# mLSTM head ends: two-step denominators, mean of the head norm on GpSimd, one more pause ahead of the transposes

## The chip, the cores and the metric

The kernel runs on one core of a Trainium2 chip. The metric is the device time of one execution in microseconds (us), given as the median of several runs. The engines are TensorE (PE; its weight loads are shown apart as PEld), VectorE (DVE), ScalarE (ACT), GpSimd (POOL) and SyncE (SP), which issues transfers. Each engine works through its own instructions in order, and semaphores tie the engines together.

## The reference

One layer of a bidirectional encoder on 512 tokens of width 1024, float32 in and out. A normed input goes through one projection whose columns are shared by four HGRN2 heads and four mLSTM heads. Each runs forward and backward over the sequence, each head's result is normed and gated, and an out-projection joins them. Cross-attention to 256 memory tokens and a squared-ReLU MLP follow. The parts that the change touches are these:

```python
def head_rmsnorm(h, g, n_heads):
    ...
    h32 = h32 * lax.rsqrt(jnp.mean(h32 * h32, axis=-1, keepdims=True) + NORM_EPS)

# mlstm_scan
den = jnp.sum(scores, axis=-1) + w_inter * jnp.einsum('bhtd,bhd->bht', qc, n_st)
h_out = num / jnp.maximum(jnp.abs(den), jnp.exp(-m_t))[..., None]

# reference
x = x + token_mixer(rmsnorm(x, norm_mix[l]), ...)
x = x + cross_attention(rmsnorm(x, norm_xattn[l]), rmsnorm(mem, norm_mem[l]), ...)
x = x + squared_relu_mlp(rmsnorm(x, norm_mlp[l]), ...)
```

## The kernel before, in words

Every large product is made of three matmuls (`mm3`, lines 261 to 263): both operands are split into a high and a low part, and high by high, high by low and low by high are summed in PSUM. Weights stream from memory through SyncE's queue, and later ones through GpSimd's (L1102), as blocks of 128 x 1024 into `st` or other buffers. `split_out` (L258) makes their high part `wh` on ScalarE and their low part `wl` on VectorE. There are three buffers each of `st`, `wh` and `wl`. Projections accumulate in four PSUM banks named `mm`; everything small uses four banks named `sm`.

The heads are Python generators. They wait in a list, `chains`; `tick()` is called at fixed places inside the projections and advances one of the first two chains to its next `yield`. A `yield` is thus a pause, in which the program places projection matmuls. Heads run in pairs: HGRN2 0 and 1, 2 and 3, then mLSTM 0 and 1 (here heads 4 and 5) and mLSTM 2 and 3 (heads 6 and 7). The first mLSTM pair runs beside the key and value projections of the memory, the second beside those and the out-projection's first part, where `drain()` finishes them. From what is written, a scheduler sets the final order of instructions on each engine by its own estimates, so an edit in one place can move instructions elsewhere.

An mLSTM chain adds masks and takes exponentials of its gates (L777 to L787), makes scores and states (L793 to L815), and then goes through four tiles of 128 tokens, `wt`. For each, the group of matmuls at L827 writes numerator and denominator of both directions to PSUM. L832 to L834 form max(|den|, e) on VectorE, L836 takes the reciprocal, L838 (ScalarE) and L839 (VectorE) scale and add the two directions. There is a pause after every second tile. Then `head_out` ends the head, as it does for the HGRN2 heads: ScalarE squares each tile and sums it (L592), `rstd_of` makes the mean on VectorE (L197) and its power -0.5 on GpSimd (L199), VectorE multiplies (L594), a pause follows, TensorE transposes four tiles (L601), VectorE applies gain and gate (L602), and the result is split for the out-projection.

`rstd_of` has ten uses: the eight heads, with four numbers on each partition, and the two tiles of memory rows, with one. For the latter ScalarE sums squares (L906), VectorE adds two halves (L908), `rstd_of` follows, VectorE scales the 128 x 1024 tile (L910), and TensorE transposes it (L919).

Of the kernel before, what the change touches and what calls it, by code (L numbers as in the profile page):

```python
# [14 lines left out]
ALU = mybir.AluOpType  # L15
# [10 lines left out]
EPS = 1e-6  # L26
# [54 lines left out]
def trunk(ctx: ExitStack, tc: tile.TileContext, x, mem, wpk, vec, cst, lmask, rmask, rows, out):  # L81
# [5 lines left out]
    v, sc, gp, pe = nc.vector, nc.scalar, nc.gpsimd, nc.tensor  # L87
# [12 lines left out]
    def smb():  # L100
        return pss.tile([P, 512], F32, tag="sm", name=nm("sm"))
# [92 lines left out]

    def rstd_of(ss, w, n):
        ms = tiny(w)
        v.tensor_scalar(out=ms, in0=ss, scalar1=1.0 / n, scalar2=EPS, op0=ALU.mult, op1=ALU.add)  # L197
        r = tiny(w)
        gp.tensor_tensor(out=r, in0=ms, in1=nh.to_broadcast([P, w]), op=ALU.pow)  # L199
        return r, ms  # L200
# [385 lines left out]
    def head_out(o, gate, gcol, idx):  # L586

        junk = T2()
        ss = tiny(4)
        for t in range(4):  # L590
            z = slice(t * P, t * P + P)
            sc.activation(junk[:, z], o[:, z], AF.Square, accum_out=ss[:, t:t + 1])  # L592
        r, _ = rstd_of(ss, 4, P)
        v.tensor_tensor(out=o[:, 0:512].rearrange("p (t e) -> p t e", e=P),  # L594
                        in0=o[:, 0:512].rearrange("p (t e) -> p t e", e=P),
                        in1=r.unsqueeze(2).to_broadcast([P, 4, P]), op=ALU.mult)
        yield
        ps = smb()
        for t in range(4):
            z = slice(t * P, t * P + P)  # L600
            pe.transpose(ps[:, z], o[:, z], ident)  # L601
        v.scalar_tensor_tensor(out=gate, in0=ps, scalar=vc[:, gcol:gcol + 1], in1=gate, op0=ALU.mult, op1=ALU.mult)  # L602
        ys[idx] = hl(YT1())
        split_out(ys[idx][0], ys[idx][1], gate)
        yield
# [161 lines left out]
    def mlstm_chain(h, gate):  # L767
# [7 lines left out]
        for dr in range(2):  # L775
# [5 lines left out]
                            in1=cm.unsqueeze(1).to_broadcast([P, 4, P]), op=ALU.add)  # L781
# [16 lines left out]
        for dr in range(2):  # L798
            v.tensor_tensor(out=kw(dr).rearrange("p (w e) -> p w e", e=P), in0=ap(pk, dr * P, [P, 3], [1, P]),
                            in1=ex(0, dr, dr, h, 3).unsqueeze(2).to_broadcast([P, 3, P]), op=ALU.mult)  # L800
# [18 lines left out]
        for wt in range(4):  # L819
# [9 lines left out]
            e2 = ap(em, wt * 8 + h, [4, 2], [1, 1])  # L829
            nd = tiny(2)  # L830
            n3 = nd[:, :].unsqueeze(2)
            v.tensor_scalar(out=n3, in0=den, scalar1=-1.0, scalar2=None, op0=ALU.mult)  # L832
            v.tensor_tensor(out=n3, in0=n3, in1=den, op=ALU.max)
            v.tensor_tensor(out=n3, in0=n3, in1=e2, op=ALU.max)  # L834
            rd = tiny(2)
            v.reciprocal(rd, nd)  # L836
            z = slice(wt * P, wt * P + P)
# [62 lines left out]
    for t in range(2):  # L900
# [6 lines left out]
        ss = tiny(1)  # L907
# [555 lines left out]
```

## Time and profile before

| | |
|---|---|
| median of three runs | 829.23 us (829.09 to 829.29) |
| profiled execution | 829.61 us, of which the span from first to last instruction is 827.6 us |
| TensorE busy | 814.7 us, 98% of the span |
| VectorE, ScalarE, GpSimd busy | 590.6, 435.2, 77.7 us |
| mean granted TensorE clock | 0.997 |

Busy time counts an engine's instructions but not its waiting. A wait is put down to the instruction that ended it, as the profile infers from semaphores. L numbers are lines of the kernel. The HGRN2 heads end between about 145 and 225 us from the start of the span, the memory rows are normed near 232 us, heads 4 and 5 end near 289 to 296 us, and heads 6 and 7 near 334 to 341 us.

### The profile page before, as it was taken

How to read it: one execution, taken by the hardware profiler on the slowest of the kernel's cores; microseconds unless marked ns; L12 is line 12 of the kernel's file. 1: busy time of each engine (PE TensorE's matmuls, PEld its weight loads, DVE VectorE, ACT ScalarE, POOL GpSimd, SP SyncE). 2: the span in 40 equal slices, each digit the busy share in tenths (PEclk: the TensorE clock that was granted, in tenths of full speed). 3: DMA queues.
4: the chain of work that ended last, by engine and by line, in shares of the span. 5: the costliest groups of instructions: out<-in, count | busy, mean ns of one | idle time of the engine just before them, and what ended most of it. 6: DMA issues, size and time to landing. Idle time of an engine off the chain costs nothing.

```text
span 827.6 us, 12644 instructions
## 1 busy us (share of the span) xinstructions
PE 814.7 (98%) x4862; PEld 677.0 (82%) x4862; DVE 590.6 (71%) x1046; ACT 435.2 (53%) x791; POOL 77.7 (9%) x131
## 2 busy tenths in 40 slices
PE   8999999999999999999999999999999999999996
PEld 6788778877878988887888888888888888888885
DVE  6568975699479888545668985676568566756685
ACT  5247574546578485445455575443454345434544
POOL 2000000100010000100100004012102210220001
PEclk9999999999999999999999999999999999999998
DMA  7332223322342334532343349969836982798332
GB/s 277 118 116 94 78 79 104 101 88 81 102 128 77 128 128 152 148 96 89 106 124 72 83 126 305 254 166 272 224 101 182 280 207 94 187 295 204 105 74 101
DMA packets 34125, 118.91 MB, mean 144 GB/s; under 512 B 3921, under 2 KB 4049, under 8 KB 34066
## 3 DMA queue, kind: packets, MB, share of 16 engines
q1 hardware_dynamic: 22832, 77.80, 27.6%
q0 software_dynamic: 10944, 39.85, 21.7%
q8 instruction: 38, 0.62, 0.3%
q10 hardware_dynamic: 290, 0.47, 0.2%
q14 instruction: 21, 0.17, 0.1%
HBM read 116.00 MB, written 2.10 MB: 143 GB/s over the span
## 4 chain that ended last, share of the span: by engine, by line
PE 85%; issue 6%; DVE 5%; ACT 2%; DMA 1%; POOL 1%; POOLq 0%; ACTq 0%; DVEq 0%
PE mm L261 17%; PE mm L263 17%; PE mm L262 17%; PE sm L1154 6%; PE sm L1155 6%; PE sm L1153 6%; PE mm L1154 2%; PE mm L1153 2%; PE mm L1155 2%; PE sm L827 1%; DVE wl L258 1%; PE sm L562 1%; PE sm L485 1%; ACT wh L258 1%; PE sm L263 1%
## 5 line engine op out<-in xcount | busy, mean ns | idle before, releaser
L258 ACT ACTIVATE wh<-st 128x1024 fp32r<-128x1024 f32 x131 | 138.7, 1060 | 185.0 <-PE mm L262 117.4
L261 PE MATMUL mm<-xT,wh 128*128 128x512 f32 x544 | 215.5, 397 | 0.0
L258 DVE TENSOR_TENSOR wl<-st,wh 128x1024 fp32r<-128x1024 f32 x131 | 160.1, 1223 | 77.3 <-ACT wh L258 76.8
L263 PE MATMUL mm<-xT,wl 128*128 128x512 f32 x544 | 212.9, 391 | 0.1
L262 PE MATMUL mm<-xT,wh 128*128 128x512 f32 x544 | 212.5, 391 | 0.2 <-DVE xT L975 0.2
L263 PEld LDWEIGHTS mm<-xT,wl 128*128 128x128 f32 x544 | 102.2, 188 | 21.8 <-DVE wl L258 0.3
L262 PEld LDWEIGHTS mm<-xT,wh 128*128 128x128 f32 x544 | 102.3, 188 | 20.8 <-DVE xT L975 0.9
L261 PEld LDWEIGHTS mm<-xT,wh 128*128 128x128 f32 x544 | 102.2, 188 | 20.8 <-ACT wh L258 0.3
L1102 POOL DMA_DIRECT2D as<-in_wpk x52 | 39.6, 763 | 250.0 <-DVE wl L258 165.0
L1342 DVE SCALAR_TENSOR_TENSOR t<-mm,rg 128x512 f32<-128x512 f32 x32 | 22.0, 690 | 52.2 <-PE mm L263 52.0
L1155 PE MATMUL sm<-wh,yT 128*128 128x512 f32 x128 | 49.8, 389 | 0.0
L1154 PE MATMUL sm<-wl,yT 128*128 128x512 f32 x128 | 49.8, 389 | 0.0
L1153 PE MATMUL sm<-wh,yT 128*128 128x512 f32 x128 | 49.8, 389 | 0.0
L258 ACT ACTIVATE wh<-as 128x1024 fp32r<-128x1024 f32 x26 | 27.6, 1062 | 37.0 <-PE sm L1155 23.7
L258 DVE TENSOR_TENSOR wl<-as,wh 128x1024 fp32r<-128x1024 f32 x26 | 31.9, 1225 | 14.0 <-ACT wh L258 14.0
L1153 PE MATMUL sm<-wh,a 128*128 128x512 f32 x84 | 32.9, 391 | 0.0
L1155 PE MATMUL sm<-wh,a 128*128 128x512 f32 x84 | 32.7, 390 | 0.0
L1154 PE MATMUL sm<-wl,a 128*128 128x512 f32 x84 | 32.7, 389 | 0.0
L1285 DVE TENSOR_TENSOR vv<-vv,sm 128x512 f32<-128x512 f32 x48 | 31.0, 680 | 1.7 <-PE sm L1155 1.7
L199 POOL TENSOR_TENSOR tiny<-tiny,misc 128x4 f32<-128x4 f32 (+1 forms) x10 | 9.6, 963 | 201.9 <-DVE tiny L197 136.7
L1153 PEld LDWEIGHTS sm<-wh,yT 128*128 128x128 f32 x128 | 24.0, 188 | 5.0
L1155 PEld LDWEIGHTS sm<-wh,yT 128*128 128x128 f32 x128 | 24.0, 188 | 5.0
(329 smaller groups left out, 1572.4 us busy)
## 6 DMA issues: line engine op xcount, KB each, us to landing
st<-in_wpk SPq DMA_DIRECT2D x131, 512.0 KB, 3.4
as<-in_wpk POOLq DMA_DIRECT2D x52, 512.0 KB, 6.5
gate<-in_wpk POOLq DMA_DIRECT2D x24, 512.0 KB, 7.2
as<-in_x SPq DMA_DIRECT2D x4, 512.0 KB, 6.7
vv<-in_x SPq DMA_DIRECT2D x8, 256.0 KB, 3.9
out<-vv SPq DMA_DIRECT2D x7, 256.0 KB, 2.2
a<-in_mem SPq DMA_DIRECT2D x2, 512.0 KB, 3.8
t<-in_rows SPq DMA_DIRECT2D x2, 256.0 KB, 5.6
```

The source lines that it names most:

```text
L199: gp.tensor_tensor(out=r, in0=ms, in1=nh.to_broadcast([P, w]), op=ALU.pow)
L258: return sc.activation(dst_hi, src, AF.Copy), v.tensor_tensor(out=dst_lo, in0=src, in1=dst_hi.bitcast(F32), op=ALU.subtract)
L261: pe.matmul(ps, lhsT=ah, rhs=bh, start=first, stop=False)
L262: pe.matmul(ps, lhsT=ah, rhs=bl, start=False, stop=False)
L263: pe.matmul(ps, lhsT=al, rhs=bh, start=False, stop=last)
L485: mm = pe.matmul(ps[b * i:b * i + b, z:z + b], lhsT=kc[j][:, w * P + b * i:w * P + b * i + b], rhs=rhs(j, w * P, i), start=True, stop=True)
L1102: return gp.dma_start(out=dst, in_=wpk[idx], **kw)
L1153: pe.matmul(ps, lhsT=ah, rhs=bh, start=new, stop=False, **fl)
L1154: pe.matmul(ps, lhsT=ah, rhs=bl, start=False, stop=False, **fl)
L1155: pe.matmul(ps, lhsT=al, rhs=bh, start=False, stop=end and k == 1, **fl)
L1285: added = v.tensor_tensor(out=z, in0=z, in1=ps, op=ALU.add if sign > 0 else ALU.subtract)
L1342: v.scalar_tensor_tensor(out=y, in0=ps, scalar=0.0, in1=rrow[:, 0:512], op0=ALU.max, op1=ALU.mult)
```

## The change

The mean in `rstd_of` is issued on GpSimd, for all ten uses. `head_out` has a second pause ahead of the transposes for the mLSTM heads (`idx` 4 to 7). The three VectorE steps of the denominators become two, a fused multiply by -1 with maximum against `e2`, and a maximum against `den`, in sixteen places.

```diff
--- before.py
+++ after.py
@@ -194,7 +194,7 @@
 
     def rstd_of(ss, w, n):
         ms = tiny(w)
-        v.tensor_scalar(out=ms, in0=ss, scalar1=1.0 / n, scalar2=EPS, op0=ALU.mult, op1=ALU.add)
+        gp.tensor_scalar(out=ms, in0=ss, scalar1=1.0 / n, scalar2=EPS, op0=ALU.mult, op1=ALU.add)
         r = tiny(w)
         gp.tensor_tensor(out=r, in0=ms, in1=nh.to_broadcast([P, w]), op=ALU.pow)
         return r, ms
@@ -595,6 +595,8 @@
                         in0=o[:, 0:512].rearrange("p (t e) -> p t e", e=P),
                         in1=r.unsqueeze(2).to_broadcast([P, 4, P]), op=ALU.mult)
         yield
+        if idx >= 4:
+            yield
         ps = smb()
         for t in range(4):
             z = slice(t * P, t * P + P)
@@ -829,9 +831,8 @@
             e2 = ap(em, wt * 8 + h, [4, 2], [1, 1])
             nd = tiny(2)
             n3 = nd[:, :].unsqueeze(2)
-            v.tensor_scalar(out=n3, in0=den, scalar1=-1.0, scalar2=None, op0=ALU.mult)
+            v.scalar_tensor_tensor(out=n3, in0=den, scalar=-1.0, in1=e2, op0=ALU.mult, op1=ALU.max)
             v.tensor_tensor(out=n3, in0=n3, in1=den, op=ALU.max)
-            v.tensor_tensor(out=n3, in0=n3, in1=e2, op=ALU.max)
             rd = tiny(2)
             v.reciprocal(rd, nd)
             z = slice(wt * P, wt * P + P)
```

The lines behind shift by up to two: transposes L603, gate L604, the numerator group L829, its scale and add L839 and L840, transposes of memory rows L920.

The change moves instructions at three places that the prediction speaks of. In the rows below, the part ahead of `<-` is what is written and what follows is read; numbers behind a name tell buffers apart and differ between the two programs.

First, GpSimd's queue at the memory rows, before:

```order
L199 TENSOR_TENSOR tiny_2321<-tiny_2319,misc 128x4
L1102 DMA gate_4206<-in_wpk 128x1024
L199 TENSOR_TENSOR tiny_2419<-tiny_2417,misc 128x1
L199 TENSOR_TENSOR tiny_2432<-tiny_2430,misc 128x1
L1102 DMA gate_4206<-in_wpk 128x1024
```

and now:

```order
L199 TENSOR_TENSOR tiny_2321<-tiny_2319,misc 128x4
L1103 DMA gate_4190<-in_wpk 128x1024
L197 TENSOR_SCALAR tiny_2417<-tiny_2415 128x1
L199 TENSOR_TENSOR tiny_2419<-tiny_2417,misc 128x1
L197 TENSOR_SCALAR tiny_2430<-tiny_2428 128x1
L199 TENSOR_TENSOR tiny_2432<-tiny_2430,misc 128x1
```

The two means stand in GpSimd's queue, each ahead of its power and behind the weight transfer. TensorE's queue at the same place, where `a_300` and `a_301` are the two memory tiles, before:

```order
L919 MATMUL sm_2454<-cs,a_300_2407 128x128
L261 MATMUL mm_2485<-xT_105,wh_2325 128x512
L262 MATMUL mm_2485<-xT_105,wh_2325 128x512
L919 MATMUL sm_2439<-cs,a_301_2408 128x128
L919 MATMUL sm_2444<-cs,a_301_2408 128x128
L919 MATMUL sm_2449<-cs,a_301_2408 128x128
L919 MATMUL sm_2454<-cs,a_301_2408 128x128
L263 MATMUL mm_2485<-xT_105,wl_2326 128x512
```

and now:

```order
L920 MATMUL sm_2454<-cs,a_300_2407 128x128
L261 MATMUL mm_2485<-xT_105,wh_2325 128x512
L920 MATMUL sm_2439<-cs,a_301_2408 128x128
L920 MATMUL sm_2444<-cs,a_301_2408 128x128
L920 MATMUL sm_2449<-cs,a_301_2408 128x128
L920 MATMUL sm_2454<-cs,a_301_2408 128x128
L262 MATMUL mm_2485<-xT_105,wh_2325 128x512
L263 MATMUL mm_2485<-xT_105,wl_2326 128x512
```

The transposes of the second tile moved ahead of one matmul of the projection beside them.

Second, the end of heads 4 and 5, VectorE, before (`t_378` is the result of head 4, `t_385` that of head 5):

```order
L839 SCALAR_TENSOR_TENSOR t_385_2822<-sm_2919,tiny_2927,t_385_2822 128x128
L602 SCALAR_TENSOR_TENSOR rg_2155<-sm_3005,vc,rg_2155 128x512
L197 TENSOR_SCALAR tiny_2981<-tiny_2976 128x4
L258 TENSOR_TENSOR a_372_2761<-mm_3089,a_372_2761 128x256
L594 TENSOR_TENSOR t_385_2822<-t_385_2822,tiny_2983 128x512
L258 TENSOR_TENSOR wl_3187<-st_3133,wh_3186 128x1024
```

and now:

```order
L840 SCALAR_TENSOR_TENSOR t_385_2820<-sm_2900,tiny_2908,t_385_2820 128x128
L840 SCALAR_TENSOR_TENSOR t_385_2820<-sm_2912,tiny_2919,t_385_2820 128x128
L594 TENSOR_TENSOR t_378_2782<-t_378_2782,tiny_2950 128x512
L258 TENSOR_TENSOR a_372_2761<-mm_3017,a_372_2761 128x256
L258 TENSOR_TENSOR wl_3109<-st_3066,wh_3108 128x1024
L594 TENSOR_TENSOR t_385_2820<-t_385_2820,tiny_2975 128x512
```

The norms (L594) of both heads now stand close together, and a low part of a weight block, `wl_3109`, stands directly ahead of that of head 5. TensorE's queue there, at the transposes of head 5 (`t_385`), before:

```order
L263 MATMUL mm_3192<-a_315_2436,wl_3084 128x256
L261 MATMUL mm_3192<-a_316_2437,wh_3083 128x256
L262 MATMUL mm_3192<-a_316_2437,wh_3083 128x256
L601 MATMUL sm_3028<-cs,t_385_2822 128x128 x4
L777 MATMUL sm_3071<-ar,selr 128x512
L777 MATMUL sm_3117<-ar,selr 128x512
```

and now:

```order
L262 MATMUL mm_3114<-a_317_2438,wh_3011 128x256
L263 MATMUL mm_3114<-a_317_2438,wl_3012 128x256
L261 MATMUL mm_3114<-a_317_2438,wh_3011 128x256
L603 MATMUL sm_3053<-cs,t_385_2820 128x128 x4
L779 MATMUL sm_3096<-ar,selr 128x512
L262 MATMUL mm_3114<-a_317_2438,wh_3011 128x256
```

These transposes, row 1244 of the queue before, are row 1228 now. Those of head 4 moved from row 1217 to row 1212.

Third, the join of heads 6 and 7 with the out-projection, TensorE's queue, before (`yT_2350` and `yT_2372` are results of HGRN2 heads, `yT_3011` is that of head 4, `t_485` the normed head 7):

```order
L262 MATMUL mm_3572<-wl_3496,yT_1642 128x512
L263 MATMUL mm_3572<-wh_3495,yT_1642 128x512
L601 MATMUL sm_3612<-cs,t_485_3381 128x128 x4
L261 MATMUL mm_3569<-wh_3524,yT_2350 128x512
L262 MATMUL mm_3569<-wl_3525,yT_2350 128x512
L263 MATMUL mm_3569<-wh_3524,yT_2350 128x512
```

and now (`yT_3036` and `yT_3059` are the results of heads 4 and 5, `yT_3623` is that of head 6):

```order
L262 MATMUL mm_3534<-wl_3475,yT_2372 128x512
L263 MATMUL mm_3534<-wh_3474,yT_2372 128x512
L603 MATMUL sm_3617<-cs,t_483_3367 128x128 x4
L603 MATMUL sm_3626<-cs,t_493_3409 128x128 x4
L261 MATMUL mm_3531<-wh_3535,yT_3036 128x512
L262 MATMUL mm_3531<-wl_3536,yT_3036 128x512
L263 MATMUL mm_3531<-wh_3535,yT_3036 128x512
L261 MATMUL mm_3531<-wh_3535,yT_3059 128x512
L262 MATMUL mm_3531<-wl_3536,yT_3059 128x512
L263 MATMUL mm_3531<-wh_3535,yT_3059 128x512
L261 MATMUL mm_3531<-wh_3587,yT_3623 128x512
L262 MATMUL mm_3531<-wl_3588,yT_3623 128x512
```

Before, 30 matmuls stood between the transposes of head 7 and the first reader of the result of head 6 (`yT_3597`); now the transposes of both heads stand together, six matmuls ahead of that reader.

## The prediction

> **What bounds the kernel now.** I read the page's engine table first, then the chain of work that ended last, then the list of what the matmul queue waited for, then the stages in windows, then the timeline around the touched places.
>
> ```profile
> PE 814.7 (98%) x4862; PEld 677.0 (82%) x4862; DVE 590.6 (71%) x1046; ACT 435.2 (53%) x791; POOL 77.7 (9%) x131
> ...
> PE 85%; issue 6%; DVE 5%; ACT 2%; DMA 1%; POOL 1%; POOLq 0%; ACTq 0%; DVEq 0%
> ```
>
> TensorE is busy for 814.7 of 827.6 us, and 85% of the chain lies on it. VectorE (71%) and GpSimd (9%) have room. An edit on them moves the time only where TensorE stands still for them, or where it makes TensorE stand still.
>
> ```profile
> PE sm L601 <- DVE t L594: 1.1, 2, 0.6
> ```
>
> Of the waits of the matmul queue only this row is one the change aims at: twice the transposes of a head (L601) wait for its norm (L594). The columns are us in total, times, longest.
>
> ```profile
> 226.00:240.00 14.00, 13.74 (x70) 10.89 (x70) 10.52 (x22) 10.79 (x23) 2.94 (x6) 1.00 0.40 117
> ...
> 268.00:295.00 27.00, 26.17 (x216) 25.30 (x214) 23.24 (x71) 15.02 (x41) 2.05 (x2) 1.00 0.36 120
> 295.00:330.00 35.00, 34.61 (x210) 30.19 (x211) 30.77 (x81) 23.80 (x66) 1.01 (x1) 1.00 0.45 144
> 330.00:345.00 15.00, 15.00 (x72) 12.41 (x71) 8.73 (x13) 6.43 (x12) 1.62 (x2) 1.00 0.47 156
> ```
>
> Columns: stretch, length, then busy time with instruction count of PE, PEld, DVE, ACT, POOL, then clock, DMA share, GB/s. Norm of the memory rows (226 to 240), heads 4 and 5 (268 to 295), heads 6 and 7 (295 to 330), the join with the out-projection (330 to 345): TensorE idles 0.26, 0.83, 0.39 and 0.00 us. The clock is 1.00 in all, so this is waiting and not throttling. What can be gained is therefore under 2 us of 829; what can be lost is open.
>
> **The denominators.** Three VectorE steps become two, sixteen times.
>
> ```profile
> L834 DVE TENSOR_TENSOR tiny<-tiny,em 128x2 f32<-128x2 f32 x16 | 2.5, 154 | 0.1
> ...
> L832 DVE TENSOR_SCALAR tiny<-sm 128x2 f32<-128x2 f32 x16 | 2.3, 143 | 1.1 <-PE sm L827 1.1
> ```
>
> A step is 143 to 154 ns, so VectorE is freed of 16 x 0.15 = 2.4 us. The new fused step reads PSUM and SBUF, which no row shows at this size; L834 (154) is the nearest, with 0.14 to 0.2 as ends. All of it lies on an engine that is 77 to 88% busy in these windows and ahead of TensorE by the sums below; on the path it is worth at most one step, 0.15 us, at the end of each pair of heads. I book it inside the sums.
>
> **The mean moves to GpSimd.** Ten uses: eight heads with four numbers per partition, two memory tiles with one.
>
> ```profile
> L197 DVE TENSOR_SCALAR tiny<-tiny 128x4 f32<-128x4 f32 (+1 forms) x10 | 1.6, 163 | 4.2 <-ACT t L592 4.2
> ...
> L199 POOL TENSOR_TENSOR tiny<-tiny,misc 128x4 f32<-128x4 f32 (+1 forms) x10 | 9.6, 963 | 201.9 <-DVE tiny L197 136.7
> ...
> L725 POOL MEMSET ex<- 128x8 f32 x2 | 0.2, 113 | 56.9 <-DVE ex L722 56.9
> ```
>
> VectorE loses 10 x 0.16 = 1.6 us, worth nothing since it is not the bound. The chain of each norm loses 0.16 plus a hand-over to GpSimd of 0.09 (289.02 + 0.17 to 289.28 below) and gains a GpSimd step plus a hand-over of that queue to itself, since the power (L199) then waits for its own engine's result. No row shows a multiply-add on GpSimd. Ends: 0.11 (memset, the smallest GpSimd step, which reads nothing) and 1.02 (the power on four). I take 0.35: the power costs 1.02 on four numbers and 0.55 on one, so 0.16 a number over a base of 0.4, and a multiply-add is nearest to that base. Undisturbed, a head's chain then grows by 0.35 + 0.09 - 0.16 - 0.09 = about 0.2 us.
>
> GpSimd is also slowed by VectorE (timeline rows: start, length, engine, line; in brackets the idle time before and who ended it):
>
> ```profile
> 821.15 0.55 POOL L1302 TENSOR_TENSOR tiny<-tiny,misc 128x1 f32<-128x1 f32 x1 [2.81 <-DVE tiny L1299]
> ```
>
> ```profile
> 147.43 1.02 POOL L199 TENSOR_TENSOR tiny<-tiny,misc 128x4 f32<-128x4 f32 x1 [74.70 <-DVE tiny L197]
> ...
> 149.95 0.69 DVE L472 TENSOR_TENSOR t<-a 128x512 f32<-128x512 f32 x1
> 150.12 1.39 POOL L199 TENSOR_TENSOR tiny<-tiny,misc 128x4 f32<-128x4 f32 x1 [1.68 <-DVE tiny L197]
> ```
>
> The same power took 1.02 alone and 1.39 beside L472, with which it overlapped from 150.12 to 150.64: 0.37 of 0.52 us, or 71% of the overlap, came on top. I use 71% for a small GpSimd step that starts beside such a VectorE instruction. The Trainium skill ("SBUF — State Buffer", section "Who interferes with whom") is stricter: a VectorE instruction with two SBUF inputs contends with a GpSimd instruction that reads SBUF, and one in a two-port mode locks the shared ports for its whole length. With 100% in place of 71% the sum at the end would be about 0.6 us more, some 831.4; the 71% of the row speaks for the lower figure.
>
> **Place 1, the memory rows.**
>
> ```profile
> 231.65 0.74 POOL L1102 DMA_DIRECT2D gate<-in_wpk  x1 [6.32 <-DVE tiny L197]
> ...
> 232.41 0.59 POOL L199 TENSOR_TENSOR tiny<-tiny,misc 128x1 f32<-128x1 f32 x1
> ...
> 233.03 0.75 DVE L910 TENSOR_SCALAR a<-a,tiny 128x1024 f32<-128x1024 f32 x1 [0.39 <-POOL tiny L199]
> ...
> 233.71 0.14 DVE L197 TENSOR_SCALAR tiny<-tiny 128x1 f32<-128x1 f32 x1
> ...
> 233.93 0.56 POOL L199 TENSOR_TENSOR tiny<-tiny,misc 128x1 f32<-128x1 f32 x1 [0.93 <-DVE tiny L197]
> ...
> 234.52 0.75 DVE L910 TENSOR_SCALAR a<-a,tiny 128x1024 f32<-128x1024 f32 x1 [0.67 <-POOL tiny L199]
> ...
> 235.33 0.66 PE L919 MATMUL sm<-cs,a 128*128 128x128 f32 x4 [0.26 <-DVE a L910]
> ```
>
> Before, the mean of tile 1 hid under the weight transfer issued from GpSimd (0.74). After, mean and power of both tiles queue behind it: mean at 232.41, power at 232.85, so the first scale (L910) starts 0.44 later, about 233.47. The second mean comes off GpSimd's queue at about that moment, beside the 0.75 us scale. Undisturbed it ends at 233.85, the power at 234.5, and the second scale starts where it did. Held for 71% of 0.75, everything is 0.53 later. The second set of transposes also stands one 128x512 matmul earlier now, 0.21 us of cover less (15.00 us over 72 instructions in the last window). So TensorE falls behind by 0.25 or by 0.75; I take 0.75, because the step starts together with the scale and not behind it. Ends: 0.1 (memset price) and 1.4 (0.65 more for a mean as dear as the power).
>
> **Place 2, heads 4 and 5, and the pause.**
>
> ```profile
> 281.29 0.28 PE L261 MATMUL mm<-a,wh 128*128 128x256 f32 x1
> ...
> 281.73 0.46 PE L827 MATMUL sm<-vv,as 128*128 128x129 f32 x2 [0.16 <-DVE tiny L833]
> ...
> 289.02 0.17 DVE L197 TENSOR_SCALAR tiny<-tiny 128x4 f32<-128x4 f32 x1
> ...
> 289.28 1.04 POOL L199 TENSOR_TENSOR tiny<-tiny,misc 128x4 f32<-128x4 f32 x1 [31.05 <-DVE tiny L834]
> ...
> 290.32 0.28 PE L263 MATMUL mm<-a,wl 128*128 128x256 f32 x1
> 290.35 0.69 DVE L594 TENSOR_TENSOR t<-t,tiny 128x512 f32<-128x512 f32 x1 [0.89 <-POOL tiny L199]
> ...
> 291.19 0.63 PE L601 MATMUL sm<-cs,t 128*128 128x128 f32 x4 [0.59 <-DVE t L594]
> ...
> 293.22 1.06 ACT L258 ACTIVATE wh<-st 128x1024 fp32r<-128x1024 f32 x1
> ...
> 293.51 1.01 POOL L199 TENSOR_TENSOR tiny<-tiny,misc 128x4 f32<-128x4 f32 x1 [3.19 <-DVE tiny L197]
> ...
> 294.53 0.28 PE L261 MATMUL mm<-a,wh 128*128 128x256 f32 x1
> 294.55 0.69 DVE L594 TENSOR_TENSOR t<-t,tiny 128x512 f32<-128x512 f32 x1 [0.80 <-POOL tiny L199]
> 294.65 0.28 PE L262 MATMUL mm<-a,wh 128*128 128x256 f32 x1
> ...
> 295.39 0.63 PE L601 MATMUL sm<-cs,t 128*128 128x128 f32 x4 [0.46 <-DVE t L594]
> ```
>
> Matmuls start 0.12 apart here (294.53, 294.65). The stalls by starts are 291.19 - 290.32 - 0.12 = 0.75 at head 4, 295.39 - 294.65 - 0.12 = 0.62 at head 5, and 281.73 - 281.29 - 0.12 = 0.32 before an L827 group. The pause was to put more matmuls between norm and transposes. But the new order also advances the chains: all L827 groups stand 4 to 5 rows earlier, head 4's transposes 5 rows earlier, and head 5's 16 rows earlier. The pause is thus eaten by the earlier slot: 16 x 0.12 = 1.92 us less work stands ahead of head 5's transposes.
>
> Its chain starts earlier too, by less. Walking the new order with these durations, head 5's transposes come at 293.15 undisturbed, which against 295.39 less 1.92 leaves TensorE 0.32 ahead. But the low part of a weight block (L258 on VectorE, two SBUF inputs, 1.22 us by its rows) now stands directly ahead of head 5's norm and starts as GpSimd takes the mean: 71% of 1.22 = 0.87 more, so 294.02 to 294.1 and TensorE +0.55 to +0.63 behind. Head 4 alone gives +0.1; since the later event sets the lag, the pair counts as +0.55. Ends: -0.32 and +1.2 (mean at 1.02).
>
> **Place 3, heads 6 and 7, and the join.** Following each wait of the second pair through the new order, I find margins of 0.2 to 1.1 us on TensorE and no new stall; +0.1 for the thinnest of them, ends 0 and 0.3. At the join the transposes of both heads now stand together, with six matmuls (6 x 0.21 = 1.3 us) ahead of the first that reads their result.
>
> ```profile
> 337.84 0.60 PE L601 MATMUL sm<-cs,t 128*128 128x128 f32 x4
> ...
> 338.48 0.75 DVE L602 SCALAR_TENSOR_TENSOR gate<-sm,vc,gate 128x512 f32<-128x512 f32 x1 [0.40 <-PE sm L601]
> ...
> 339.18 1.23 DVE L258 TENSOR_TENSOR wl<-st,wh 128x1024 fp32r<-128x1024 f32 x1
> 339.26 0.63 ACT L258 ACTIVATE yT<-gate 128x512 fp32r<-128x512 f32 x1
> ```
>
> From transposes to the high part took 0.64 + 0.75 + 0.63 = about 2.0 us. Matmuls of neighbouring tiles fill part of the gap; I book +0.2, ends 0 and 0.7 (2.0 less 1.3). The HGRN heads 0 to 3 get the dearer mean without the pause; their transposes never appear in the list of waits beyond the two above, so their 0.2 us stays hidden, and if that cover went each would cost 0.2. SyncE's queue changes by one pair of loads of the residual passing two weight loads, whose three buffers hold; nothing is booked.
>
> **Sum.** 0.75 + 0.55 + 0.1 + 0.2 = +1.6 us against the profiled execution: span 827.6 becomes 829.2, its time 829.61 becomes 831.2. The profiled execution lies 0.38 above the median of 829.23, so the median would be 830.8.
>
> **The rivals.** *Cheap and undisturbed.* The mean costs nearer 0.11 and no VectorE instruction holds it: 0.1 to 0.25 at the memory rows, -0.32 at head 5, +0.1 at the join: about 0, 829.2. For it: GpSimd is nearly idle. Against it: the 1.39 us row.
>
> *The pause works.* If the mean takes under about 0.2 us and the norms finish before their slots, all three stalls of place 2 vanish: 0.75 + 0.62 + 0.32 = 1.69, giving 827.5, faster. It decides only if head 5's norm is done 0.6 us earlier than my walk has it. For it: VectorE is 4 us lighter. Against it: the 16 rows.
>
> *The mean is as dear as the power* (1.02). Place 1 gives +1.4, place 2 +1.2, or +2 where the mean of head 4 is held too, place 3 +0.6 to +0.9: +3.2 to +4.3, about +3.8, 833.0. For it: base and setup dominate the power at one number too (0.55). Against it: a power is many steps, a multiply-add one.
>
> **How the numbers follow.** 0.2%, about 1.66 us, is what a measurement can tell from no change here: 827.57 to 830.89. My forecast (830.8, its own range 830.0 to 831.6) gets 0.42, half on each side of that bound; cheap and undisturbed 0.30; the pause works 0.10, all faster; the dear mean 0.18, all slower. So faster 0.10, same 0.30 + 0.21 = 0.51, slower 0.21 + 0.18 = 0.39. The range from 828.4 to 832.9 leaves out the faster case and half of the dear one.
>
> **What the profile after would show.** Mean: a GpSimd row of about 0.35, or 0.7 and more beside an L910 or a weight split. Place 1: the second L919 set near 236.0, with a longer wait for L910. Place 2: head 5's transposes near 294.1, still waiting for the norm; gone from the list of waits if the pause works. Join: a TensorE gap of 0.2 for the gated output. I am wrong if the mean is far from 0.35, if the scheduler's order meets other transfers, or if GpSimd's step waits for nothing beside VectorE.

## The result, and the profile after

The changed kernel takes 830.24 us (median of 22 runs, 829.89 to 830.78) against 829.16 for the kernel before (22 runs, 828.92 to 829.40). The ratio is 1.0013, with a 95% interval of 1.0007 to 1.0019: 1.08 us slower, resolved, and within the 0.2% that the prediction called no change. The profiled execution took 829.89 us, its span is 828.1 us.

The page of the changed kernel, busy time and the chain that ended last:

```profile
PE 814.2 (98%) x4862; PEld 676.2 (82%) x4862; DVE 587.9 (71%) x1020; ACT 435.3 (53%) x791; POOL 81.9 (10%) x141
...
PE 86%; issue 5%; DVE 4%; ACT 2%; POOL 1%; DMA 1%; POOLq 0%; ACTq 0%; DVEq 0%
```

VectorE lost 2.7 us of work, GpSimd gained 4.2, and TensorE still bounds. What the matmul queue waited for, after, and then the one row of before that answers to its last (us in total, times, longest):

```profile
PE sm L603 <- DVE t L594: 1.1, 2, 0.6
...
PE sm L920 <- DVE a L911: 0.8, 2, 0.5
```

```profile
PE sm L919 <- DVE a L910: 0.3, 1, 0.3
```

The waits of heads 4 and 5 at their transposes are as long as before. That of the memory rows grew by 0.5 us. The stages (windows; columns as in the prediction):

```profile
226.00:240.00 14.00, 13.20 (x68) 10.56 (x67) 9.87 (x19) 10.92 (x23) 3.89 (x8) 1.00 0.46 115
...
268.00:295.00 27.00, 25.63 (x212) 24.82 (x211) 23.00 (x62) 13.90 (x40) 3.60 (x4) 1.00 0.36 119
295.00:330.00 35.00, 35.00 (x209) 30.11 (x208) 28.46 (x63) 23.81 (x58) 0.00 (x0) 1.00 0.42 138
330.00:345.00 15.00, 15.00 (x79) 12.68 (x77) 7.90 (x17) 7.04 (x20) 2.66 (x4) 1.00 0.39 136
```

TensorE idles 0.80 us at the memory rows (0.26 before). In 268 to 295 it idles 1.37 us (0.83 before), in 295 to 330 nothing (0.39 before), because head 5's wait now falls ahead of 295 and not behind: the sum of the two is 1.37 against 1.22. At the join it shows no idle time; busy time hides small delays, though, since a matmul's row overlaps the next one's, and the starts show them better.

Spans alone mislead here, since the two profiled executions did not start alike. It is better to take matmuls at the same place in TensorE's queue and compare their starts. Three of them, before and after, in the timeline (start, length): ahead of the memory rows, ahead of heads 4 and 5, and inside the out-projection, behind the join with heads 6 and 7.

```profile
209.22 0.48 PE L261 MATMUL mm<-xT,wh 128*128 128x512 f32 x1
...
269.63 0.28 PE L261 MATMUL mm<-a,wh 128*128 128x256 f32 x1
...
370.88 0.39 PE L263 MATMUL mm<-wh,yT 128*128 128x512 f32 x1
```

```profile
208.56 0.48 PE L261 MATMUL mm<-xT,wh 128*128 128x512 f32 x1
...
269.50 0.28 PE L261 MATMUL mm<-a,wh 128*128 128x256 f32 x1
...
371.02 0.39 PE L263 MATMUL mm<-wh,yT 128*128 128x512 f32 x1
```

The differences are -0.66, -0.13 and +0.14. The changed kernel's profiled execution was 0.66 us ahead when it came to the memory rows (0.5 of it already in the first 24 us, which the change does not touch), lost 0.53 there and 0.27 from heads 4 to the join. A fourth mark, L1155 at 489.97 us before and 490.08 after, shows no more loss. So up to there the trace puts 0.53 + 0.27 - 0.03 = 0.77 us on the change; the medians say 1.08. The rest comes at the end of the program. From there to the last matmul the two run alike, and the last matmul starts at 819.83 before and 819.94 after; but behind it GpSimd's closing steps, which end the program, take longer (line 1459 before and 1460 after; number of steps, shortest, median and longest in ns, and the starts of the first and the last of them in us; before first):

```profile
L1459 POOLq EVENT_SEMAPHORE  x4: 17/17/17, 826.9 to 827.5; - x4
...
L1459 POOLq EVENT_SEMAPHORE_RANGE_CLEAR  x1: 142/142/142, 827.2 to 827.2; - x1
```

```profile
L1460 POOLq EVENT_SEMAPHORE  x4: 17/17/17, 826.9 to 828.0; - x4
...
L1460 POOLq EVENT_SEMAPHORE_RANGE_CLEAR  x1: 142/142/142, 827.2 to 827.2; - x1
```

Up to the clearing of the semaphores the two go alike. The last step then starts at 827.5 before and at 828.0 after. Counted from the end of the last matmul, the span ends 7.38 us later before and 7.78 after: 0.40 us more, which together with the 0.77 makes 1.17. The start-up differs by some tenths from execution to execution and drops out of this count.

The 0.27 can be placed more closely by two more matmuls at the same place in the queue, one at 298.43 before and 298.26 after, the other at 311.42 and 311.46. From the second mark to 298 us, past the transposes of heads 4 and 5, the change loses nothing and gains 0.04. It loses 0.20 from there to 311, where heads 6 and 7 begin, gives back 0.04 until 332, and loses 0.15 from 332 to the third mark, at the join. What it loses at the join is a wait for the gated result of a head, as the timeline of the changed kernel shows:

```profile
345.41 0.69 DVE L258 TENSOR_TENSOR yT<-gate,yT 128x512 fp32r<-128x512 f32 x1
...
345.87 0.39 PE L262 MATMUL mm<-wl,yT 128*128 128x512 f32 x1
...
346.15 0.73 PE L263 MATMUL mm<-wh,yT 128*128 128x512 f32 x2
...
346.73 0.39 PE L261 MATMUL mm<-wh,yT 128*128 128x512 f32 x1
```

Matmuls of this size start 0.23 apart. From 345.87 to 346.73 lie three steps, 0.86 in place of 0.69: the first L263 starts 0.05 behind the end of the split that it reads.

The two rows on GpSimd of the head norm and the memory norm (mean of one in ns; 4 numbers per partition eight times, 1 number twice):

```profile
L199 POOL TENSOR_TENSOR tiny<-tiny,misc 128x4 f32<-128x4 f32 (+1 forms) x10 | 10.2, 1017 | 0.8
L197 POOL TENSOR_SCALAR tiny<-tiny 128x4 f32<-128x4 f32 (+1 forms) x10 | 3.5, 346 | 202.6 <-ACT t L592 202.5
```

A mean costs 346 ns on average, but the average is of two kinds: six of the ten take 0.19 or 0.20 us, the others 0.42, 0.45, 0.69 and 0.75. The timeline at the memory rows shows one of each:

```profile
230.99 0.74 POOL L1103 DMA_DIRECT2D gate<-in_wpk  x1 [6.24 <-DVE tiny L909]
...
231.81 0.19 POOL L197 TENSOR_SCALAR tiny<-tiny 128x1 f32<-128x1 f32 x1
...
232.08 0.57 POOL L199 TENSOR_TENSOR tiny<-tiny,misc 128x1 f32<-128x1 f32 x1
...
232.68 0.75 DVE L911 TENSOR_SCALAR a<-a,tiny 128x1024 f32<-128x1024 f32 x1 [0.68 <-POOL tiny L199]
232.73 0.75 POOL L197 TENSOR_SCALAR tiny<-tiny 128x1 f32<-128x1 f32 x1
...
233.56 0.56 POOL L199 TENSOR_TENSOR tiny<-tiny,misc 128x1 f32<-128x1 f32 x1
...
234.16 0.75 DVE L911 TENSOR_SCALAR a<-a,tiny 128x1024 f32<-128x1024 f32 x1 [0.72 <-POOL tiny L199]
...
234.97 0.65 PE L920 MATMUL sm<-cs,a 128*128 128x128 f32 x4 [0.49 <-DVE a L911]
```

The first mean takes 0.19 us, the second 0.75: it starts 0.05 us behind the first tile's scale on VectorE and ends 0.05 behind the scale's end. In before's time (0.66 later) the second transposes start at 235.63 in place of 235.33, so 0.30 later, and they stand one matmul earlier (0.23): 0.53.

At heads 4 and 5 the timeline of the changed kernel is:

```profile
287.06 1.23 DVE L258 TENSOR_TENSOR wl<-st,wh 128x1024 fp32r<-128x1024 f32 x1 [0.44 <-ACT wh L258]
...
287.92 0.42 POOL L197 TENSOR_SCALAR tiny<-tiny 128x4 f32<-128x4 f32 x1 [29.82 <-ACT t L592]
...
289.44 0.28 PE L261 MATMUL mm<-a,wh 128*128 128x256 f32 x1
...
290.25 0.66 PE L603 MATMUL sm<-cs,t 128*128 128x128 f32 x4 [0.53 <-DVE t L594]
290.31 0.19 POOL L197 TENSOR_SCALAR tiny<-tiny 128x4 f32<-128x4 f32 x1 [0.84 <-ACT t L592]
290.44 1.21 DVE L258 TENSOR_TENSOR wl<-st,wh 128x1024 fp32r<-128x1024 f32 x1
290.58 1.94 POOL L199 TENSOR_TENSOR tiny<-tiny,misc 128x4 f32<-128x4 f32 x1
...
292.42 0.28 PE L261 MATMUL mm<-a,wh 128*128 128x256 f32 x1
292.56 0.69 DVE L594 TENSOR_TENSOR t<-t,tiny 128x512 f32<-128x512 f32 x1 [0.91 <-POOL tiny L199]
293.31 0.66 PE L603 MATMUL sm<-cs,t 128*128 128x128 f32 x4 [0.61 <-DVE t L594]
```

At head 4 the mean was caught by the end of a low part of a weight block (0.42 us, ending 0.05 behind it). At head 5 the mean escaped (0.19 us, over just as the next low part starts) and the power was caught: 1.94 us where 1.01 to 1.05 is its undisturbed length, for 1.07 us of overlap with L258. The gaps between starts at the transposes are 0.81 and 0.89, less 0.12 for a matmul: stalls of 0.69 and 0.77 against 0.75 and 0.62 before.

All the caught steps lose by one measure, the overlap less 0.14 us. The means at 149.26, 232.73, 287.92 and 332.57 us overlapped a VectorE instruction by 0.64, 0.70, 0.37 and 0.40 and took 0.50, 0.56, 0.23 and 0.26 longer than 0.19; head 5's power overlapped by 1.07 and took 0.93 longer than 1.01. In each of these the VectorE instruction began first and read SBUF alone. Beside one that reads PSUM nothing is lost: before, head 5's power at 293.51 took its 1.01 us beside an L258 that splits a projection.

### The profile page after: what moved, and what is told of

It reads as the page before. It is cut to its first block, busy times and chain, and to the rows that moved or that the text cites. A ratio compares the mean times of both kernels' runs of the same rounds, so it can differ in the third digit from the quotient of the medians.

```text
span 828.1 us, 12631 instructions
## 1 busy us (share of the span) xinstructions
PE 814.2 (98%) x4862; PEld 676.2 (82%) x4862; DVE 587.9 (71%) x1020; ACT 435.3 (53%) x791; POOL 81.9 (10%) x141
## 4 chain that ended last, share of the span: by engine, by line
PE 86%; issue 5%; DVE 4%; ACT 2%; POOL 1%; DMA 1%; POOLq 0%; ACTq 0%; DVEq 0%
PE mm L261 18%; PE mm L262 17%; PE mm L263 17%; PE sm L1154 6%; PE sm L1156 6%; PE sm L1155 6%; PE mm L1154 2%; PE mm L1156 2%; PE mm L1155 2%; PE sm L829 1%; PE sm L562 1%; PE sm L485 1%; ACT wh L258 1%; DVE wl L258 1%; PE sm L263 1%
## 5 line engine op out<-in xcount | busy, mean ns | idle before, releaser
L258 ACT ACTIVATE wh<-st 128x1024 fp32r<-128x1024 f32 x131 | 138.7, 1060 | 185.2 <-PE mm L262 116.6
L258 DVE TENSOR_TENSOR wl<-st,wh 128x1024 fp32r<-128x1024 f32 x131 | 160.1, 1223 | 75.2 <-ACT wh L258 74.5
L263 PE MATMUL mm<-xT,wl 128*128 128x512 f32 x544 | 212.7, 391 | 0.1
L263 PEld LDWEIGHTS mm<-xT,wl 128*128 128x128 f32 x544 | 102.1, 188 | 21.9 <-DVE wl L258 0.3
L1155 PE MATMUL sm<-wl,yT 128*128 128x512 f32 x128 | 49.8, 389 | 0.0
L258 ACT ACTIVATE wh<-as 128x1024 fp32r<-128x1024 f32 x26 | 27.6, 1062 | 37.0 <-PE sm L1156 23.7
L258 DVE TENSOR_TENSOR wl<-as,wh 128x1024 fp32r<-128x1024 f32 x26 | 31.9, 1226 | 14.0 <-ACT wh L258 14.0
L1155 PE MATMUL sm<-wl,a 128*128 128x512 f32 x84 | 32.7, 389 | 0.0
L1155 PEld LDWEIGHTS sm<-wl,yT 128*128 128x128 f32 x128 | 24.0, 188 | 5.0
```

Source lines behind the costliest of these rows:

```text
L258: return sc.activation(dst_hi, src, AF.Copy), v.tensor_tensor(out=dst_lo, in0=src, in1=dst_hi.bitcast(F32), op=ALU.subtract)
L263: pe.matmul(ps, lhsT=al, rhs=bh, start=False, stop=last)
L1155: pe.matmul(ps, lhsT=ah, rhs=bl, start=False, stop=False, **fl)
```

## The experiments

Each kernel was timed beside the kernel before in five rounds. The intervals of one such run are about 0.001 wide to either side, which is as large as the effects; the traces resolve them better. "Memory", "heads" and "later" are the changes, against before, of the start of the same matmul from the first to the second mark above, from the second to the third, and from the third to the fourth, in us; the start-up drops out. "Heads" thus reaches from heads 4 and 5 through heads 6 and 7 to the join. "End" is the change of the time from the end of the last matmul to the end of the span. Theory A and theory B are stated in the first expectation.

| kernel | median, of before beside it | ratio (95%) | memory | heads | later | end |
|---|---|---|---|---|---|---|
| the change | 830.24, 829.16 | 1.0013 (1.0007 to 1.0019) | +0.53 | +0.27 | -0.03 | +0.40 |
| pause only | 829.37, 829.18 | 1.0001 (0.9992 to 1.0010) | 0.00 | +0.08 | -0.01 | -0.06 |
| mean only | 830.78, 829.18 | 1.0017 (1.0009 to 1.0026) | +0.58 | +0.70 | +0.01 | +0.37 |
| denominators only | 829.63, 829.18 | 1.0004 (0.9995 to 1.0013) | +0.02 | +0.36 | +0.25 | -0.08 |
| change without mean | 829.01, 829.18 | 0.9997 (0.9988 to 1.0007) | 0.00 | -0.20 | -0.07 | -0.08 |
| the same again | 828.93, 829.17 | 0.9998 (0.9989 to 1.0007) | +0.01 | -0.17 | -0.05 | -0.07 |
| change without pause | 830.49, 828.91 | 1.0018 (1.0010 to 1.0027) | +0.59 | +0.40 | +0.24 | +0.47 |
| memory mean on VectorE | 829.39, 828.91 | 1.0006 (0.9997 to 1.0015) | -0.01 | +0.24 | 0.00 | +0.29 |
| head mean on VectorE | 829.19, 828.91 | 1.0003 (0.9995 to 1.0012) | +0.57 | -0.18 | -0.02 | +0.03 |
| memory scale on ScalarE | 830.14, 828.91 | 1.0014 (1.0005 to 1.0023) | -0.24 | +1.12 | +0.01 | +0.25 |
| no mean step | 828.57, 829.17 | 0.9992 (0.9984 to 1.0001) | -0.44 | -0.06 | -0.03 | 0.00 |
| norm in halves | 830.11, 829.17 | 1.0010 (1.0001 to 1.0019) | +0.16 | +0.53 | 0.00 | +0.28 |
| no mean step, memory only | 828.48, 829.03 | 0.9993 (0.9984 to 1.0002) | -0.28 | -0.26 | -0.07 | -0.05 |

The last column falls into two groups, 0.25 to 0.47 and -0.08 to 0.03. In the first, the trace has 197 to 202 records of GpSimd, its semaphore steps and drains among them; in the second it has 187 to 191. Before has 189, and the ten means make 199. In each of the six kernels of the first group the 197th record starts 0.3 us late, whichever of the closing steps that is; in three of them it is a drain, which then takes 0.19 us in place of 0.05. The other kernels have no 197th. So ten more instructions on GpSimd cost the change 0.40 us at the end of the program, where TensorE has long been done. Why the 197th is late no run shows. Marks and end added up agree with the medians within 0.2 us in every row, within 0.1 for the change.

**Pause only.** Edit, against before:

```diff
         yield
+        if idx >= 4:
+            yield
         ps = smb()
```

> Only the second pause, mean on VectorE and three-step denominators as before. Theory A (the loss is the mean on GpSimd: its place in GpSimd's queue and the ports it shares with VectorE): no change, 829.2 within 0.3, and the two waits of heads 4 and 5 at the transposes stay near 0.6 and 0.5 us, since their place in TensorE's queue is unchanged (rows 1217 and 1244). Theory B (the loss is the order: transposes put where less work stands ahead of them): the pause moves only heads 6 and 7, to the join, and costs 0.2 to 0.5 us there, 829.4 to 829.7.

It took 829.37 us, 0.19 above before and within the interval of no change. The transposes of heads 4 and 5 wait as before (list of waits of this kernel):

```profile
PE sm L603 <- DVE t L594: 1.1, 2, 0.6
```

In TensorE's queue they stand at rows 1217 and 1244, exactly where they stood. The pause moved only heads 6 and 7, from rows 1409 and 1422 to 1445 and 1446, and that cost less than 0.1 us. Theory A holds. The pause does nothing at the two waits that a pause could shorten.

**Mean only.** Edit, against before:

```diff
-        v.tensor_scalar(out=ms, in0=ss, scalar1=1.0 / n, scalar2=EPS, ...
+        gp.tensor_scalar(out=ms, in0=ss, scalar1=1.0 / n, scalar2=EPS, ...
```

> Only the mean on GpSimd. Theory A: nearly the whole loss, 829.9 to 830.4: about 0.5 us at the memory rows (the second mean takes 0.75 us beside the scale of the first tile) and 0.2 to 0.5 at heads 4 and 5. Theory B: about 0.3 us, since head 5 moves 5 rows and not 16: 829.4 to 829.6.

830.78 us, ratio 1.0017: above both ranges, and more than the whole change. The memory rows lose 0.58, as in the change; heads 4 and 5 lose 0.70. Their waits in this kernel:

```profile
PE sm L601 <- DVE t L594: 1.0, 1, 1.0
...
PE sm L601 <- DVE tiny L836: 0.8, 1, 0.8
```

Together 1.8 us against 1.1. The powers took 1.05 and 1.01 here, undisturbed: with the three-step denominators the weight block does not fall beside them. So a head's loss needs no VectorE instruction beside GpSimd's: both means took 0.19 too. What is left is the step, its hand-over and the order that it brings (head 5's transposes five rows earlier).

**Denominators only.** Edit, against before:

```diff
-            v.tensor_scalar(out=n3, in0=den, scalar1=-1.0, scalar2=None, op0=ALU.mult)
+            v.scalar_tensor_tensor(out=n3, in0=den, scalar=-1.0, in1=e2, op0=ALU.mult, op1=ALU.max)
             v.tensor_tensor(out=n3, in0=n3, in1=den, op=ALU.max)
-            v.tensor_tensor(out=n3, in0=n3, in1=e2, op=ALU.max)
```

> Only the two-step denominators. Theory A: no loss, 828.9 to 829.3; head 5's transposes stand 10 rows earlier, but its chain is earlier too. Theory B: the 10 rows cost, a wait at head 5 near 1.2 us in place of 0.5, 829.6 to 830.0.

829.63 us, at the lower edge of theory B's range, with no change inside the interval. By its mechanism theory B was wrong all the same, and theory A was right about heads 4 and 5 alone: head 5's stall did not grow (0.54 by starts against 0.62; with head 4's, 1.38 against 1.37). The 0.36 holds a new wait at the join, 0.50 by starts, which the timeline of this kernel shows:

```profile
335.74 0.68 DVE L258 TENSOR_TENSOR a<-mm,a 128x512 fp32r<-128x512 f32 x1
335.75 0.40 PE L263 MATMUL mm<-wh,yT 128*128 128x512 f32 x1
...
336.48 0.50 PE L261 MATMUL mm<-wh,yT 128*128 128x512 f32 x1 [0.33 <-DVE a L258]
```

A split of a finished projection (L258 to `a`) stands on VectorE behind the norm of head 6 and a weight block, and the next matmul waits for it. Before, the same split started at 335.35 and no matmul waited. Another 0.25 is lost behind the out-projection, at 382 to 387 us; 0.10 of it is a longer wait of TensorE for VectorE's `xT` (0.50 by starts against 0.40). With fewer VectorE steps TensorE waited longer.

**The change without the mean on GpSimd.** Edit, against the change: the mean's line of `rstd_of` back to VectorE.

```diff
-        gp.tensor_scalar(out=ms, in0=ss, scalar1=1.0 / n, scalar2=EPS, ...
+        v.tensor_scalar(out=ms, in0=ss, scalar1=1.0 / n, scalar2=EPS, ...
```

> The changed kernel with the mean back on VectorE (pause and two-step denominators stay). Theory A: the loss is gone, 828.9 to 829.4. Theory B: most of it stays, 829.7 to 830.2.

829.01 us, and 828.93 in a second run whose expectation follows; the loss is gone, as theory A has it. By the marks pause and two steps together gain 0.2 to 0.3 us, which the timing can't resolve from nothing.

> The kernel of the fourth run again (mean on VectorE, pause, two-step denominators), to compare on the same chip with the two others: by its first trace 0.28 us below before, 828.8 to 829.2. Rival: no gain at all, 829.2 to 829.5.

**The change without the pause.** Edit, against the change:

```diff
-        if idx >= 4:
-            yield
```

> The changed kernel without the second pause. The order at heads 4 and 5 is the same with and without it (rows 1212 and 1228), so the stalls there should stay near 0.6 and 0.7 us. Theory A (the pause acts only on heads 6 and 7, and there takes away a wait at the join that the two-step denominators bring, as in the run with them alone, 0.5 us near 336): 830.5 to 830.9, 0.3 to 0.6 above the changed kernel. Theory B (the pause does nothing or harms): 830.0 to 830.3.

830.49 us, just below theory A's range (830.5 to 830.9) by time; against its own before the loss is 1.58, where the change has 1.08. The trace says that the pause saves 0.40 - 0.27 = 0.13 at the heads and the join and 0.27 behind. Rows 1212 and 1228 stay, and so do the stalls of heads 4 and 5. The wait at the join is back, 0.3 us in place of the 0.5 of the denominators alone. The use of the pause is that it takes back what the two-step denominators brought, some 40 us behind the place where it was wanted.

**Memory mean on VectorE, and head mean on VectorE.** Edits, against the change:

```diff
-        gp.tensor_scalar(out=ms, ...
+        (v if w == 1 else gp).tensor_scalar(out=ms, ...
```

```diff
-        gp.tensor_scalar(out=ms, ...
+        (gp if w == 1 else v).tensor_scalar(out=ms, ...
```

> The changed kernel with the mean of the two memory tiles on VectorE, that of the heads on GpSimd. Theory A (half of the loss and more is the memory rows): 0.55 us less than the changed kernel, 829.5 to 829.8; waits of L920 back to 0.2 and 0.4 by starts. Theory B (the loss is at the heads): 830.0 to 830.3.

> The changed kernel with the mean of the heads on VectorE, that of the memory tiles on GpSimd. Theory A: the memory rows keep their 0.55 us, the heads lose little: 829.4 to 829.9. Theory B (the loss is at the heads): 829.0 to 829.3.

829.39 and 829.19 us. The first is just below its range, and the trace shows the 0.53 at the memory rows gone and the 0.24 at the heads kept. The second falls into theory B's range by its time, and the trace tells why neither theory had it whole: it keeps 0.57 at the memory rows, as theory A says, and gains 0.18 at the heads, where the change loses 0.27. So the mean on GpSimd costs some 0.55 at the memory rows and 0.45 at the heads, halves rather than nearly all at the one, and the end on top. The two places are independent in these runs: what stands at the one doesn't change what is lost at the other.

The 0.45 is spread. Against the kernel with the head mean on VectorE, the change has lost 0.15 us by 298 us, behind the transposes of head 5, another 0.25 by 311, at the first matmuls of heads 6 and 7, and 0.05 from there to the third mark. At the second mark the two stand at 269.50 and 269.39, 0.11 apart. At the L799 matmuls of the second pair they are 0.41 apart (the change first):

```profile
308.19 0.49 PE L799 MATMUL sm<-yT 128*128 128x128 f32 x2
```

```profile
307.78 0.62 PE L799 MATMUL sm<-yT 128*128 128x128 f32 x4
```

What holds the first matmuls of heads 6 and 7 is not shown. By times alone (0.48 and 0.28 above before, intervals of 0.8 us to either side) this would not have been decided.

**Memory scale on ScalarE.** Edit, against the change:

```diff
-        v.tensor_scalar(out=a, in0=a, scalar1=r, scalar2=None, op0=ALU.mult)
+        sc.activation(a, a, AF.Copy, scale=r)
```

> The changed kernel with the scale of the memory tiles (128x1024, two of them) on ScalarE in place of VectorE, about 1.06 us each by the weight splits of that size. If VectorE's scale held the second mean by the shared ports, that mean takes about 0.19 us now in place of 0.75. If it was slow for another reason (first power still finishing, cold code), it stays near 0.75. The total is not the point: ScalarE is 0.3 us slower a tile and has other work, so 829.8 to 831.

The timeline of this kernel at the second mean:

```profile
232.53 1.15 ACT L911 ACTIVATE a<-a,tiny 128x1024 f32<-128x1024 f32 x1 [0.90 <-POOL tiny L199]
232.58 0.19 POOL L197 TENSOR_SCALAR tiny<-tiny 128x1 f32<-128x1 f32 x1
232.85 0.56 POOL L199 TENSOR_TENSOR tiny<-tiny,misc 128x1 f32<-128x1 f32 x1
```

With the same scale on another engine the mean starts at the same point of the chain and takes 0.19 in place of 0.75. It was VectorE's scale that held it, and nothing on GpSimd. The Trainium skill ("SBUF — State Buffer", section "Who interferes with whom") says that VectorE in a two-port mode, when it issues first, has the shared ports for the whole instruction and blocks GpSimd, and that `tensor_scalar` can enter such a mode. The second mean of the change agrees in that it ends only behind the scale; by 0.05 us, though, and not by its own 0.19. That the scale ran in such a mode is not shown apart from this. The total, 830.14, is no gain, since 1.12 us are lost at the heads: this order puts head 5's transposes at row 1215, and the means of heads 4 and 5 are caught in it (0.68 and 0.69 us).

**No mean step.** Edit, against the change:

```diff
-            sc.activation(junk[:, z], o[:, z], AF.Square, accum_out=ss[:, t:t + 1])
+            sc.activation(junk[:, z], o[:, z], AF.Square, scale=P ** -0.5, accum_out=ss[:, t:t + 1])
...
-        gp.tensor_scalar(out=ms, in0=ss, ...
-        gp.tensor_tensor(out=r, in0=ms, in1=nh.to_broadcast([P, w]), op=ALU.pow)
+        gp.tensor_tensor(out=r, in0=ss, in1=nh.to_broadcast([P, w]), op=ALU.pow)
```

(and a scale of 1/32 on the squares of the memory rows).

> The changed kernel without any mean step: ScalarE's squares are scaled so that their sum is the mean, and the power on GpSimd reads it directly. The constant 1e-6 of the norm is left out. If the price of the mean on GpSimd is what the change lost, the memory rows are at or below their stalls of before (0.16 and 0.44 by starts) and heads 4 and 5 lose some 0.2 us less each: 828.3 to 829.0. Rival (the power of head 5 is still held by the low part of a weight block, and that is the larger part at the heads): head 5's stall stays at 0.5 to 0.7, 829.0 to 829.5.

828.57 us: the memory rows gain 0.44 against before, 0.97 against the change. At the heads it gains only 0.06 against before, and the rival of its expectation is what the timeline of this kernel shows at head 5 (L197 is the power here):

```profile
289.35 1.22 DVE L256 TENSOR_TENSOR wl<-st,wh 128x1024 fp32r<-128x1024 f32 x1
289.48 1.95 POOL L197 TENSOR_TENSOR tiny<-tiny,misc 128x4 f32<-128x4 f32 x1 [1.11 <-ACT t L590]
```

Without any mean the power still runs into the weight block, overlaps it by 1.09 us and takes 1.95. Removing 0.19 us of work ahead of it does not help head 5 as long as the order puts the two side by side: its stall is 0.79 by starts, against 0.77 in the change. What this kernel gains on the change at the heads it gains at head 4 (0.42 against 0.69).

**Norm in halves.** Edit, against the change without the mean on GpSimd: mean, power and multiply each for two tiles at a time.

```diff
+        for hf in range(2):
+            ss = tiny(2)
...
+            r, _ = rstd_of(ss, 2, P)
+            oh = o[:, hf * 256:hf * 256 + 256].rearrange("p (t e) -> p t e", e=P)
+            v.tensor_tensor(out=oh, in0=oh, in1=r.unsqueeze(2).to_broadcast([P, 2, P]), op=ALU.mult)
```

> Mean on VectorE, pause and two-step denominators as in the run without the mean on GpSimd, but the norm in two halves of two tiles: the first half's mean, power and multiply can run ahead, and behind the last sum stand a power on two numbers (about 0.7 by 0.55 for one and 1.02 for four) and a multiply of 128x256 (about 0.36) in place of 1.02 and 0.69. If the chain behind the last sum is what TensorE waits for at heads 4 and 5, their stalls (0.74 and 0.44) shrink by up to 0.64 each: 828.0 to 828.6. Rival: the order moves the transposes as far as the chain shortens, and nothing is gained: 828.8 to 829.3.

830.11 us, a miss: at heads 4 and 5 the power on two numbers took 0.70 to 0.72, the last of the four 1.00 beside a VectorE split, and the multiply 0.42 to 0.43, close to what was expected, and yet the waits grew from two of 1.1 in all (0.7 and 0.4) to

```profile
PE sm L603 <- DVE t L596: 1.5, 3, 0.6
```

The order now holds four sets of transposes in place of two (rows 1212, 1230, 1235, 1255), and TensorE waits at three of them. A shorter chain became more waits.

**No mean step for the memory rows alone.** Edit, against the change without the mean on GpSimd:

```diff
-            sc.activation(jk, a[:, c * 512:c * 512 + 512], AF.Square, accum_out=s2_[:, c:c + 1])
+            sc.activation(jk, a[:, c * 512:c * 512 + 512], AF.Square, scale=1.0 / 32, accum_out=s2_[:, c:c + 1])
...
-        r, _ = rstd_of(ss, 1, D)
+        r = tiny(1)
+        gp.tensor_tensor(out=r, in0=ss, in1=nh, op=ALU.pow)
```

> Mean of the heads on VectorE, pause and two-step denominators, and no mean step for the two memory tiles alone: their squares are scaled so that the sum is the mean, and the constant 1e-6 is left out for them. If the gains and losses read from TensorE's positions add up: -0.44 at the memory rows, -0.2 from heads 4 to the out-projection, so 0.65 below before, 828.3 to 828.7. Rival (the lead won at the memory rows is lost at heads 4 and 5, where the transposes wait for a chain that does not start earlier): 828.8 to 829.1.

828.48 us, the lowest median here; by the marks -0.28 - 0.26 - 0.07 = -0.61, where -0.65 was expected from the two places added (less at the memory rows than thought, a little more behind). Its ratio of 0.9993 has an interval that reaches 1.0002, so it is not shown to be faster than before, and it leaves a constant of the norm out. It is faster than the change.

## Why the prediction was right, and where only by luck

The forecast beside what the traces show, in us:

| term | forecast | shown |
|---|---|---|
| memory rows | +0.75 | +0.53 |
| heads 4 and 5 | +0.55 | -0.04 |
| heads 6 and 7 (298 to 332 us) | +0.1 | +0.16 |
| join (332 to 371 us) | +0.2 | +0.15 |
| behind the join | none | -0.03 |
| end of the program | none | +0.40 |
| sum | +1.6 | +1.17 (medians: 1.08) |

**The bound and the price of VectorE's time: right.** The 2.7 us that VectorE lost are nowhere to be found in the time. That only TensorE's waits move the time holds up to the last matmul and not behind it. One reading was off: VectorE is 75 to 88% busy in the windows up to 330 us and 58% in the last, not 77 to 88%; nothing hung on it.

**The price of the mean: right on average, wrong in kind.** I took 0.35 undisturbed; the mean over ten is 0.346, but undisturbed it is 0.19, and the rest is four means caught beside VectorE. The fixed part of the power was the wrong neighbour, the memset's 0.11 the nearer one.

**The shared ports: right mechanism, too small a share.** I used 71% of the overlap, from one row of 0.52 us of overlap. A share is the wrong form: that row lost 0.37, which is the overlap less 0.15, and the rows after lose the overlap less 0.14, whether it is 0.37 or 1.07. For long overlaps this comes near to the whole instruction (0.93 of 1.07 us, 87%). The 100% set beside the 71% lies above every one of these rows.

**Memory rows: +0.75 predicted, +0.53 measured.** The mechanism was right, shown by the experiments that undo it. The term was too large since the first scale started 0.31 later and not 0.44, and since the held mean took 0.75 and not 0.35 and 71% of 0.75, which is 0.88. The matmul of cover lost was worth 0.23 and not 0.21.

**Heads 4 and 5: +0.55 predicted, 0.04 gained, and the wrong instruction.** I had head 5's mean held by the weight block; it was the power behind it. Head 5's stall did grow, from 0.62 to 0.77, but head 4's shrank from 0.75 to 0.69, and 0.13 less is lost at the other matmuls of this stretch. And the step "the pause is eaten by the earlier slot" is wrong. The order of these rows does not depend on the pause at all: 1217 and 1244 before and with the pause alone, 1212 and 1228 in the change and without the pause. Mean and denominators together move head 5's by 16 rows, the denominators alone by 10, the mean alone by 5. The expected gain of the pause went nowhere, since it never acted on these heads.

**Heads 6 and 7 and the join: +0.3 predicted, +0.31 measured, half of it as told.** The join's 0.2 was a gap for the gated result, and 0.15 is what the trace has there. The walk through heads 6 and 7 found margins and no new stall; 0.20 us are lost where they begin, and what holds them there is not shown. That the pause at the join also removes a wait that the denominators bring was not in my list.

**The denominators, booked at nothing:** alone they are worth +0.6 us by the marks (+0.45 in time, not resolved). With the pause beside them the pair gains 0.2 to 0.3. The parts do not add up: pause, mean and denominators alone give 0.07 + 1.29 + 0.63 = 1.99 us by the marks, together 0.77.

**The number: in part luck.** The sum of +1.6 was for what happens up to the join, and there the trace has 0.81, half of it. The measured 830.24 lies inside the forecast's own range of 830.0 to 831.6 only because 0.40 came at the end of the program, where nothing had been booked; without it the median would be near 829.8. The wider range, 828.4 to 832.9, would have held no change at all as well. What was foreseen is the place and the cause of the largest term, the memory rows.

Three things stay open: why the 197th record of GpSimd is late, what holds the first matmuls of heads 6 and 7, and why the two-step denominators alone cost 0.25 us behind the out-projection. No run was made for any of them.

## What to carry to other kernels

Where a scheduler sets the order, look up in the order whether an edit moved the instructions that wait before costing what it does to the wait: a pause, a shorter chain and a lighter engine each left TensorE waiting as long or longer here. The pause did not touch the order at the waits it was meant for, and the other two put the transposes earlier by what the chain had gained, or by more. A small step moved from VectorE to GpSimd can cost, beside what it takes itself, nearly all that is left of the VectorE instruction it falls beside, where that one reads SBUF alone. When an effect is a tenth of a per cent, compare the start of the same matmul at a few marks in two traces, and the end behind the last matmul too; it separated 0.53, 0.27, 0.40 and the start-up, where the timing saw one number.

## What the runs showed of the hardware that I had not expected

A multiply-add on GpSimd on one or four numbers per partition takes 0.19 us undisturbed, only a little more than the 0.14 to 0.17 it took on VectorE. A GpSimd power of 1.01 us that starts 0.13 to 0.14 us behind a VectorE subtraction of two SBUF operands takes 1.94 us, and did so in the change (1.94) and without a mean step (1.95). In these traces a small GpSimd step that starts while VectorE runs an instruction on SBUF alone loses the overlap less 0.14 us, from 0.23 us lost in 0.37 to 0.93 in 1.07. And the 197th record of GpSimd's queue starts 0.3 us late in every kernel here that has one, so that ten more small instructions made the end of the program 0.40 us longer.
